# A decoder trunk step on one core: the mixer's pairs in another order, the sums of x in tiles of their own, and the first weights and last stores at other times

## The chip, the core and the metric

The kernel runs on one core of a Trainium2 chip. The core has engines that work side by side and meet at semaphores: TensorE (PE in the profile; PEld is its weight load), VectorE (DVE), ScalarE (ACT), GpSimd (POOL) and SyncE (SP). SP and POOL issue nearly all transfers; what is issued by one of them is in one queue. The metric is the time of one execution on the device in microseconds (us).

## The reference

One step of a hybrid decoder layer for 512 prompt positions and 8 sample positions, 520 columns in all:

```
proj = rmsnorm(x) @ w_in                       # 2048 -> b, c, hin, q, k, v, og, glr
cu, _ = causal_dwconv(cg * hin, conv_prev, conv_w)
ya = bg * cu                                   # 1024 channels, gated convolution
o, s_new = gla_chunked(q, k, v, logf, s0, 64)  # 4 heads, dk 128, dv 256
yb = rmsnorm_per_head(o) * silu(og)            # 1024 channels, gated attention
x = x + concat(ya, yb) @ w_out
u, v = split(rmsnorm(x) @ w_up)                # 2 x 5632
x = x + (silu(causal_dwconv(u, prev, w) + b) * v) @ w_down
y = rmsnorm(x)
```

Beside `y`, the new convolution and attention states are returned. All is float32.

## The kernel before, in words

Activations lie transposed, 128 channels by 520 columns in a tile (P = 128, T = 520, HT = 260). A float32 product is made of three matmuls on halves: `split` writes a rounded high part (ACT, L117, L105, L1166) and the rest as low part (DVE, L118, L106, L1170), and PE multiplies high by high, high by low and low by high.

The stages in order of time are these.

1. The first projections and the attention heads 0 to 3 (to about 493 us in the trace shown). Each product is a plain `group` (matmuls on L134). Beside the matmuls run the steps of the head before (`gla_head`), and in a head the gate's decay goes through ACT (L801 to L815), a scan on DVE (`bc`, L810), POOL (`e<-bc`, L227), and ACT and DVE again to `L` (L837, L840), which PE needs on L897. A scheduler orders the instructions of this stage by its own estimates.
2. Nine pairs of projection tiles, table `MIX`: `ch` is a pair of c and hin of one convolution tile, `b` two tiles of b, `og` two tiles of the gate. From here on products are made by a seven-product form (Strassen and Winograd) for blocks of two by two, products in the order `ORDER = (1, 5, 6, 2, 7, 3, 4)`. Step i is one product of 24 matmuls (`up_product`, L1190); pair n takes the steps 7n to 7n + 6, and NM = 63 is the first step of the next stage. From here on the instructions of each engine run in the order of the code.
3. "wo", the output projection: two chunks c of the 2048 input channels, four groups g of output tiles each, seven products a group (`chunk_product`, L1429; `chunk_finish` adds the products onto `acc`, on DVE at L1447, or copies on ACT at L1445).
4. "up" and "down", the feed-forward part (to about 2180 us), and the last norm.

The names the change touches:

- `mixer_sums(g)` (L665), g = 0 to 3, makes the forms 5, 4, 7, 6 of x for stage 2: four loads of x on POOL (L671, from `xT_d`), scaling on ACT (L673), sums on DVE, and a split; the result is kept (g = 0) or stored to `mt_d` by POOL (`stored`, L633). It runs beside the heads, in tiles of the pool `tmp` (eight buffers, shared with the heads). `load_mixer_sums(g)` (L694) brings the stored forms back by POOL (L697).
- `weights` (L1096) loads a pair's four weight tiles by SP: (1,1), (2,1), (2,2) at once (L1109), (1,2) later (`load_rest`, L1149). The tiles (2,k) lie in the pool `raw2`. `s` (DVE, L1112) is the first sum of two of them.
- `mixed_done` and `mix_gate` finish a pair: y tiles, their pair sums (`pair_sums`), and four stores by `stored`, which splits on ACT into a buffer `fh`, then on DVE, and then lets POOL write both halves to `g_d`. A `yield` of v in a step list means "go on at v steps after the pair's first product was followed".
- `load_form(kind, c, j)` (L615) loads the forms of product j of chunk c from `g_d`, two tiles of 260 KB for the high half (x = 0) and two for the low half (x = 1).
- `load_residual(g)` (L1395) loads the residual into `acc`; `add_residual` (L1400) adds it by accumulating transfers.
- `flat` (L577) are ten small stores of the last convolution tile's new state.

The forms of chunk 0 are loaded during the last pair, and the choice of queue is:

```python
first = kind == "wo" or c == 0 and x == 1
(nc.gpsimd if first else nc.sync).dma_start(
```

Of the kernel before, what the change touches and what calls it, by code (L numbers as in the profile page):

```python
# [9 lines left out]
F32 = mybir.dt.float32  # L10
# [3 lines left out]
ALU = mybir.AluOpType  # L14
# [23 lines left out]
def trunk_kernel(  # L38
# [565 lines left out]
    def load_form(kind, c, j):  # L604

        home = (7 * c + j) % 8
        parts_ = []
        for x in range(2):
            tiles = []
            for q in range(2):  # L610
                t = slots[2 * home + q].tile(
                    [P, T], F32R, tag=f"y{'hl'[x]}{2 * home + q}", name="form"
                )
                first = kind == "wo" or c == 0 and x == 1
                (nc.gpsimd if first else nc.sync).dma_start(  # L615
                    two(t.bitcast(F32)),
                    forms_d[kind][c][PLACE[ORDER[j]], x, 2 * q : 2 * q + 2].rearrange(
                        "i p c -> p i c"
                    ),
                )  # L620
                tiles += halves(t)
            parts_.append(tiles)
        xd[kind, c, ORDER[j]] = list(zip(*parts_))
# [41 lines left out]
    def mixer_sums(g):  # L665


        xg = [tmp()[:, :T] for _ in range(4)]
        for q, x in enumerate(xg):
            m = first_tile("mix", g, q // 2)  # L670
            nc.gpsimd.dma_start(two(x), rows_of(xT_d, "mix", g, q))  # L671
            for j, h in enumerate(halves(x)):
                nc.scalar.activation(h, h, AF.Copy, scale=gmix[:, m + j : m + j + 1])  # L673

        def out(f, t):
            if g == 0:
                split(t, *form(f, g))
            else:
                stored(t, [mt_d[f - 4, g, x] for x in range(2)], tmp())

        yield
        t1, t2 = xg[0], tmp()[:, :T]
        sub(t1, xg[0], xg[1])
        minus(t2, t1, xg[3])
        out(5, t1)
        yield
        minus(xg[2], t2, xg[2])
        out(4, t2)
        out(7, xg[2])
        yield  # L690
        sub(xg[1], xg[3], xg[1])
        out(6, xg[1])

    def load_mixer_sums(g):  # L694
        for f in (5, 4, 7, 6):
            for x, t in enumerate(form(f, g)):
                nc.gpsimd.dma_start(t.bitcast(F32), mt_d[f - 4, g, x])  # L697

    def pair_sums(he, h):

# [8 lines left out]
    with ExitStack() as mix:  # L709
# [13 lines left out]
        def mixed_done(k, y):  # L723
            if k % 2 == 0:
                return
            he, dst, i = even.pop(k - 1), g_d[k // 8], k // 2 % 4
            t21, t34 = pair_sums(he, y)
            for src, f in ((halves(he)[0], 6), (t21, 0), (t34, 2), (y, 4)):
                n = 1 if f == 6 else 2
                stored(src, [dst[f : f + n, x, i] for x in range(2)], tmp())  # L730
# [305 lines left out]
        slots[1::4] = slots[2::4] = [yt2] * 4  # L1036
        wxr = yctx.enter_context(tc.tile_pool(name="raw2", bufs=4, side="right"))
        wxp = yctx.enter_context(tc.tile_pool(name="sums", bufs=2, side="right"))
        for g in (1, 2):
            load_mixer_sums(g)  # L1040

        for j in range(2):
# [27 lines left out]

    def chunk_source(kind, w, c, g, m, k):
        c0 = first_tile(kind, g, m - 1) * P
        return w[8 * c * P : 8 * (c + 1) * P, c0 : c0 + 2 * P].rearrange(
            "(i t p) c -> t p i c", t=2, p=P
        )[k - 1]

    MIX = (
        ("ch", 4), ("ch", 5), ("b", 4), ("og", 2), ("ch", 6), ("ch", 7), ("b", 6), ("og", 4),  # L1080
        ("og", 6),
    )

    def mix_source(n, m, k):
        what, j = MIX[n]
        c0 = {"ch": 1024 * m + j * P, "b": (j + m - 1) * P, "og": 5120 + (j + m - 1) * P}[what]
        return w_in[(k - 1) * 1024 : k * 1024, c0 : c0 + P].rearrange("(k p) c -> p k c", p=P)

    def source(kind, at):
        if kind == "mix":  # L1090
# [5 lines left out]
    def weights(source, dma7):  # L1096


        raw, s = {}, wxp.tile([P, 1024], F32, tag="s", name="s", bufs=1)
        loads = []  # L1100
        for m, k in ((1, 1), (2, 1), (2, 2), (1, 2)):
            w = (wp if m == 1 else wxr).tile(
                [P, 1024], F32, tag="raw", name="raw", bufs=m + 2
            )
            src = source(m, k)
            loads.append((w.rearrange("p (k c) -> p k c", k=src.shape[1]), src))
            raw[m, k] = w
        for x in loads[:3]:
            nc.sync.dma_start(*x)  # L1109

        def plus(out, x, y):
            return lambda: nc.vector.tensor_tensor(out, x, y, op=ALU.add)  # L1112

        def dma_plus(out, x):

            return lambda: nc.gpsimd.dma_start(out, x, accum_op=ALU.add)

        src = {
            1: raw[1, 1], 2: raw[1, 2], 3: s, 4: raw[2, 2], 5: s, 6: s, 7: raw[2, 1],
        }  # L1120
        sums = {
            5: plus(s, raw[2, 2], raw[2, 1]), 6: plus(s, s, raw[1, 1]), 3: plus(s, s, raw[1, 2]),
        }
        if not dma7:
            sums[7] = plus(raw[2, 1], raw[2, 1], raw[1, 1])
        return dict(
            src=src, sums=sums, bank={}, used=set(), rest=loads[3],
            seventh=dma_plus(raw[2, 1], raw[1, 1]) if dma7 else lambda: None,
        )

# [10 lines left out]
    def begin(n):  # L1141
        kind, at = groups[n]

        state[kind, at] = weights(
            source(kind, at), kind == "up" or kind in ("mix", "wo") and at[0] > 0
        )

    def load_rest(n):
# [127 lines left out]
    def mix_gate(n):  # L1276


        st = state.pop(("mix", (n,)))
        u, v = st[2], st[7]  # L1280
        what, j = MIX[n]
        if what == "ch":
            zt = next_z()
            z = zt[:, 2 : 2 + T]
            nc.vector.scalar_tensor_tensor(z, u, -1.0, v, op0=ALU.mult, op1=ALU.mult)
            mult(z, z, R2)
            yield 1.5
# [12 lines left out]
        k = j  # L1300
        if what == "og":
            k = 8 + j
            mult(v, v, R)
            on = [tmp()[:, :T] for _ in range(2)]
            for x in range(2):
                nc.sync.dma_start(on[x], o_d[j + x])
            yield 0.5
            nc.scalar.activation(u, u, AF.Silu)
            nc.scalar.activation(v, v, AF.Silu, scale=-1.0)
            yield 3  # L1310
            mult(u, u, on[0])
            mult(v, v, on[1])
            yield 4
        dst, i = g_d[k // 8], k // 2 % 4
        t21, t34 = pair_sums(u, v)
        yield 4.5
        stored(halves(u)[0], [dst[6:7, x, i] for x in range(2)], fh())
        yield 7
        stored(v, [dst[4:6, x, i] for x in range(2)], fh())
        yield 7.5  # L1320
        stored(t21, [dst[0:2, x, i] for x in range(2)], fh())
        yield 10.5
        stored(t34, [dst[2:4, x, i] for x in range(2)], fh())

    def gate(t):
# [68 lines left out]
        for q in range(4):  # L1394
            nc.gpsimd.dma_start(two(acc[g, q]), rows_of(xT_d, "wo", g, q))  # L1395

    def add_residual(g):

        for q in range(4):
            nc.gpsimd.dma_start(  # L1400
                two(acc[g, q]), rows_of(x1_d, "down", g, q), accum_op=ALU.add
            )

    def load_last():

# [30 lines left out]
    def chunk_finish(i):  # L1436
# [3 lines left out]

        def onto(q, b, op=ALU.add):
            a = two(acc[g, q])
            if kind == "down" and c == 0 and (q, b) not in ((1, "f"), (3, "a")):
                scale = 1.0 if op == ALU.add else -1.0
                nc.scalar.activation(a, inner(bk[b]), AF.Copy, scale=scale)  # L1445
            else:
                nc.vector.tensor_tensor(a, a, inner(bk[b]), op=op)  # L1447
# [129 lines left out]
    for i, (kind, at, r) in enumerate(order):  # L1577
# [43 lines left out]
        if kind == "wo":  # L1621
# [2 lines left out]
                load_form("wo", 1, 0)  # L1624
            if c == 0 and j == 4 and g + 1 < NG:
                load_residual(g + 1)
            if c == 0 and g == NG - 1 and j >= 1:
                load_form("wo", 1, j)
            if c == 1 and g == NG - 1:
# [6 lines left out]
        if 7 * n in (NM - 7, NU - 7):  # L1636
            for x in {1: (0, 1), 2: (2, 3), 4: (4, 5), 6: (6,)}.get(j, ()):
                load_form(groups[n + 1][0], 0, x)
        if i == NM - 1:
            load_residual(0)  # L1640
        if kind == "down":
            c, g = at
            if c == 0 and g == 0 and j == 1:
# [1 line left out]
            if c == 0 and j == 0:  # L1645
                new_sums(g)
            if j == 5 and (c, g) in ((1, 0), (1, 1), (1, 2), (2, 2)):
                add_residual({0: 2, 1: 3}.get(g, c - 1))
# [143 lines left out]
```

## Time and profile before

| | |
|---|---|
| time, median of 3 runs (range) | 2253.38 us (2252.05 to 2257.63) |
| the profiled execution: its time, its span | 2252.56 us, 2250.8 us |
| busy in the span: PE, DVE, ACT, POOL | 96%, 77%, 49%, 22% |
| transfers | 426.16 MB, mean 189 GB/s |
| matmuls | 17751 |

A row of a group or of the timeline gives the start or the busy time, the line and operation, what is written and read, and in brackets how long the engine was idle before it and what ended this. "SPq" and "POOLq" are the sequencers that issue transfers. Row "x24" is 24 instructions. In a row of windows stand the stretch, its length, the busy time of PE, PEld, DVE, ACT and POOL with their counts, the granted clock of PE, the transfers' busy share and GB/s. A row of waits gives the total, the number of times and the longest, in us. In the rows of queues (q0 is POOL's, q1 SP's) stand packets, MB and the share of the 16 DMA engines. In the chain a row is start, length and what.

### The profile page before, as it was taken

Reading aid. Unit: us, or ns where it says so; the run is one execution under the profiler, and the core shown is the slowest. Engines: PE = TensorE matmul, PEld = TensorE weight load, DVE = VectorE, ACT = ScalarE, POOL = GpSimd, SP = SyncE. Lnnn points to the kernel's source line nnn. Section 1 sums busy time; section 2 is a strip of 40 time slices with the busy share of each in tenths; the row PEclk is TensorE's granted clock in tenths of the full one; section 3 lists DMA queues with packets and bytes.
Section 4 is the critical chain, followed back from the end, with each engine's and each line's share of the span. In section 5 each row is a group of like instructions: output and inputs, shape, how many; then the busy total and the mean of one; then the engine's idle time right before and its main releaser. Section 6 shows DMA issues by size and latency. Waiting matters only on the chain.

```text
span 2250.8 us, 43866 instructions
## 1 busy us (share of the span) xinstructions
PE 2171.4 (96%) x17751; PEld 2143.3 (95%) x17751; DVE 1739.4 (77%) x2290; ACT 1112.7 (49%) x1625; POOL 490.7 (22%) x687
## 2 busy tenths in 40 slices
PE   8998999989997998999999999999999999999997
PEld 7998889989997997999999999999999999999997
DVE  5365473647886897888888889888899878888876
ACT  5344453334543476655555555555555554444445
POOL 3135151341225421121221221113112311010000
PEclk9999999999998999999999999999999999999999
DMA  8344464467769799676676766766767968784734
GB/s 245 103 133 146 123 201 138 112 220 188 196 164 303 246 267 307 158 187 176 169 189 169 188 176 169 188 171 179 185 167 197 293 172 234 235 247 152 227 104 151
DMA packets 465367, 426.16 MB, mean 189 GB/s; under 512 B 22233, under 2 KB 418421, under 8 KB 465021
## 3 DMA queue, kind: packets, MB, share of 16 engines
q1 hardware_dynamic: 418193, 285.85, 44.2%
q0 software_dynamic: 45648, 135.29, 22.2%
q8 instruction: 139, 2.28, 0.4%
q10 hardware_dynamic: 1324, 2.23, 0.3%
q14 instruction: 63, 0.52, 0.1%
HBM read 304.78 MB, written 85.64 MB: 173 GB/s over the span
## 4 chain that ended last, share of the span: by engine, by line
PE 83%; DMA 6%; DVE 5%; ACT 2%; issue 2%; POOL 1%; SPq 1%; ACTq 0%; DVEq 0%; POOLq 0%
PE mm L1190 33%; PE ms L1190 13%; PE mm L134 11%; PE y L1429 8%; PE x L1429 8%; PE f L1429 3%; PE e L1429 3%; DMA t<-o_d 1%; DMA yl<-t_d 1%; DVE lo L106 1%; PE ms L897 1%; DVE lo L1170 1%; DMA vb<-v_d 1%; DMA form<-g_d 1%; DMA s<-in_state_gla_dram 1%
## 5 line engine op out<-in xcount | busy, mean ns | idle before, releaser
L1190 PE MATMUL mm<-yl,hi 128*128 128x260 f32 x1696 | 478.5, 282 | 3.5 <-DVE yl L118 2.8
L1190 PE MATMUL mm<-yh,lo 128*128 128x260 f32 x1696 | 480.1, 283 | 1.0 <-DVE lo L1170 1.0
L1190 PE MATMUL mm<-yh,hi 128*128 128x260 f32 x1696 | 479.9, 283 | 0.7 <-DMA yh<-t_d 0.5
L1166 ACT ACTIVATE hi<-raw 128x1024 fp32r<-128x1024 f32 x324 | 342.5, 1057 | 228.7 <-PE mm L1190 71.2
L1170 DVE TENSOR_TENSOR lo<-raw,hi 128x1024 fp32r<-128x1024 f32 x324 | 395.5, 1221 | 36.6 <-ACT hi L1166 36.1
L1170 DVE TENSOR_TENSOR lo<-s,hi 128x1024 fp32r<-128x1024 f32 x243 | 298.3, 1228 | 126.6 <-ACT hi L1166 121.1
L1166 ACT ACTIVATE hi<-s 128x1024 fp32r<-128x1024 f32 x243 | 257.2, 1059 | 221.3 <-DVE s L1112 85.2
L1190 PEld LDWEIGHTS mm<-yl,hi 128*128 128x128 f32 x1696 | 319.5, 188 | 4.4 <-DVE yl L118 3.0
L1190 PEld LDWEIGHTS mm<-yh,lo 128*128 128x128 f32 x1696 | 319.5, 188 | 1.2 <-DVE lo L1170 1.2
L1190 PEld LDWEIGHTS mm<-yh,hi 128*128 128x128 f32 x1696 | 319.4, 188 | 1.3 <-DMA yh<-t_d 0.7
L1190 PE MATMUL ms<-b,hi 128*128 128x260 f32 x1408 | 257.6, 283 | 0.0
L1190 PEld LDWEIGHTS ms<-b,hi 128*128 128x128 f32 x1408 | 217.8, 189 | 0.0
L1429 PE MATMUL x<-form,hi 128*128 128x260 f32 x1120 | 207.1, 285 | 10.5 <-ACT e L1453 6.9
L1429 PE MATMUL y<-form,hi 128*128 128x260 f32 x1120 | 204.6, 283 | 1.9 <-DVE acc L1447 1.9
L1112 DVE TENSOR_TENSOR s<-s,raw 128x1024 f32<-128x1024 f32 x162 | 197.8, 1221 | 2.8
L1190 PE MATMUL ms<-b,lo 128*128 128x260 f32 x704 | 198.8, 282 | 0.0
L1429 PEld LDWEIGHTS x<-form,hi 128*128 128x128 f32 x1120 | 174.1, 190 | 11.8 <-ACT e L1453 7.1
L1429 PEld LDWEIGHTS y<-form,hi 128*128 128x128 f32 x1120 | 172.4, 188 | 2.3 <-ACT hi L1166 2.3
L1429 PE MATMUL x<-form,lo 128*128 128x260 f32 x560 | 159.2, 284 | 0.0
L1429 PE MATMUL y<-form,lo 128*128 128x260 f32 x560 | 158.3, 283 | 0.0
L106 DVE TENSOR_TENSOR lo<-raw,hi 128x1024 fp32r<-128x1024 f32 x76 | 96.6, 1271 | 71.7 <-ACT hi L105 61.8
L105 ACT ACTIVATE hi<-raw 128x1024 fp32r<-128x1024 f32 x76 | 79.8, 1052 | 118.5 <-PE mm L134 112.5
(354 smaller groups left out, 5212.6 us busy)
## 6 DMA issues: line engine op xcount, KB each, us to landing
raw<-in_w_up_dram SPq DMA_DIRECT2D x176, 512.0 KB
raw<-in_w_down_dram SPq DMA_DIRECT2D x96, 512.0 KB
raw<-in_w_in_dram SPq DMA_DIRECT2D x92, 512.0 KB
form<-f_d SPq DMA_DIRECT2D x126, 260.0 KB
raw<-raw POOLq DMA_DIRECT2D x56, 512.0 KB, 5.4
f_d<-t POOLq DMA_DIRECT2D x80, 260.0 KB, 5.2
raw<-in_w_out_dram SPq DMA_DIRECT2D x32, 512.0 KB
form<-g_d POOLq DMA_DIRECT2D x56, 260.0 KB, 7.6
```

What stands on the lines that cost most here:

```text
L105: nc.scalar.activation(hi, raw, AF.Copy)
L106: nc.vector.tensor_tensor(lo, raw, hi.bitcast(F32), op=ALU.subtract)
L134: nc.tensor.matmul(o, w, xx, start=first and i == 0, stop=last and i == 2)
L897: nc.tensor.matmul(pb[:, c * 64 : (c + 1) * 64], L[:, c, :], rhs[:, c], start=True, stop=True,)
L1112: return lambda: nc.vector.tensor_tensor(out, x, y, op=ALU.add)
L1166: nc.scalar.activation(his[i], src, AF.Copy)
L1170: nc.vector.tensor_tensor(los[i], src, his[i].bitcast(F32), op=ALU.subtract)
L1190: nc.tensor.matmul(st["bank"][b], w[:, k, :], x, start=b not in st["used"] and k == 0 and j == 0, stop=k == 7 and j == 2, skip_group_check ...
L1429: nc.tensor.matmul(ps[:, m, :], w[:, k, m * P : (m + 1) * P], x, start=b not in st["used"] and k == 0 and j == 0, stop=k == 3 and j == 2, ...
```

## The change

It has these parts:

1. `MIX` goes from ch4, ch5, b4, og2, ch6, ch7, b6, og4, og6 to ch4, og2, ch5, og4, b4, og6, ch6, ch7, b6, and the gate's tiles become chunk 0 of the projection, the convolution's chunk 1 (`g_d[1 - k // 8]`, and `c = 1 - c` in `chunk_source`).
2. The four stores of the last pair come at 9.5, 13.5, 17.5 and 20.5 instead of 4.5, 7, 7.5 and 10.5.
3. The form loads of chunk 0: high halves on SP, low halves on POOL.
4. The residual of group 0 is not loaded before the first sums. Four of the six first accumulations become ACT copies; `add_residual("wo", 0)` follows in group 2.
5. `mixer_sums` uses tiles of `yt1` (name `yx`) instead of `tmp`, starts with its four loads of x, and stores all four groups; eight more stores and eight more loads.
6. `second_half` issues the two weights (2,1) and (2,2); for the first pair this happens when the pool `raw2` opens (`early`).

The core of the diff:

```diff
@@ load_form
-                first = kind == "wo" or c == 0 and x == 1
-                (nc.gpsimd if first else nc.sync).dma_start(
+                pool = x == 1 if c == 0 else kind == "wo"
+                (nc.gpsimd if pool else nc.sync).dma_start(
@@ mixer_sums
-        xg = [tmp()[:, :T] for _ in range(4)]
+        def place(n):
+            return yt1.tile([P, T], F32, tag=f"y{'hl'[n % 2]}{n // 2 * 4}", name="yx")
+        xg = [place(n) for n in range(4)]
+        for q, x in enumerate(xg):
+            nc.gpsimd.dma_start(two(x), rows_of(xT_d, "mix", g, q))
+        yield
...
-        def out(f, t):
-            if g == 0:
-                split(t, *form(f, g))
-            else:
-                stored(t, [mt_d[f - 4, g, x] for x in range(2)], tmp())
+        def out(f, t, hi):
+            stored(t, [mt_d[f - 4, g, x] for x in range(2)], hi)
...
+    def second_half(source):
+        raw = {}
+        for k in (1, 2):
+            w = raw[2, k] = wxr.tile([P, 1024], F32, tag="raw", name="raw")
+            src = source(2, k)
+            nc.sync.dma_start(w.rearrange("p (k c) -> p k c", k=src.shape[1]), src)
+        return raw
@@ after the heads
-        for g in (1, 2):
+        early = second_half(lambda m, k: mix_source(0, m, k))
+        for g in range(3):
             load_mixer_sums(g)
@@ weights
-        for x in loads[:3]:
-            nc.sync.dma_start(*x)
+        nc.sync.dma_start(*loads[0])
+        raw = {**raw, **(second or second_half(source))}
@@ mix_gate
-        dst, i = g_d[k // 8], k // 2 % 4
+        dst, i = g_d[1 - k // 8], k // 2 % 4
-        yield 4.5
+        late = n == len(MIX) - 1
+        yield 9.5 if late else 4.5
         stored(halves(u)[0], [dst[6:7, x, i] for x in range(2)], fh())
-        yield 7
+        yield 13.5 if late else 7
         stored(v, [dst[4:6, x, i] for x in range(2)], fh())
-        yield 7.5
+        yield 17.5 if late else 7.5
         stored(t21, [dst[0:2, x, i] for x in range(2)], fh())
-        yield 10.5
+        yield 20.5 if late else 10.5
         stored(t34, [dst[2:4, x, i] for x in range(2)], fh())
@@ chunk_finish
-            if kind == "down" and c == 0 and (q, b) not in ((1, "f"), (3, "a")):
+            new = kind == "down" or g == 0
+            if new and c == 0 and (q, b) not in ((1, "f"), (3, "a")):
@@ the loop over steps
+            if c == 0 and g == 2 and j == 1:
+                add_residual("wo", 0)
-        if i == NM - 1:
-            load_residual(0)
+        if i == NM:
+            new_sums(0)
```

POOL at the start of the output projection, before. `g_d_119` is chunk 0, `g_d_120` chunk 1, `acc` the residual's sums:

```order
L615 DMA form<-g_d_119 128x2x260 x16
L633 DMA g_d_119<-fh 128x2x260
L633 DMA g_d_119<-t 128x2x260
L633 DMA g_d_120<-fh 128x260
L633 DMA g_d_120<-t 128x260
L615 DMA form<-g_d_119 128x2x260 x12
L1395 DMA acc<-xT_d 128x2x260 x4
```

The same place after:

```order
L1127 DMA raw<-raw 128x1024
L615 DMA form<-g_d_119 128x2x260 x4
L577 DMA out_dram<-flat 8x128 x10
L615 DMA form<-g_d_119 128x2x260 x10
L1409 DMA acc<-xT_d 128x2x260 x4
L633 DMA g_d_120<-fh 128x260
L633 DMA g_d_120<-t 128x260
```

Half of the forms have left the queue, the last pair's stores stand behind all of them, the residual that follows them is group 1's, and the ten `flat` stores have come in between.

SP at the start of the nine pairs, before. L1109 loads (1,1), then (2,1) and (2,2); L1149 is (1,2); `t<-o_d` is an attention output for the gate:

```order
L1003 DMA o_d<-o 128x520 x2
L1109 DMA raw<-in_w_in_dram 128x8x128
L1044 DMA t<-o_d 128x520
L1109 DMA raw<-in_w_in_dram 128x8x128 x2
L1149 DMA raw<-in_w_in_dram 128x8x128
L1109 DMA raw<-in_w_in_dram 128x8x128
L1044 DMA t<-o_d 128x520
```

The same place after; L720 is `second_half`:

```order
L1027 DMA o_d<-o 128x520 x2
L1119 DMA raw<-in_w_in_dram 128x8x128
L1069 DMA t<-o_d 128x520
L1161 DMA raw<-in_w_in_dram 128x8x128
L720 DMA raw<-in_w_in_dram 128x8x128 x2
L1119 DMA raw<-in_w_in_dram 128x8x128
L720 DMA raw<-in_w_in_dram 128x8x128
L1069 DMA t<-o_d 128x520
```

The first pair's (1,2), L1161, now stands ahead of its (2,1) and (2,2), and one more weight of the second pair ahead of the second `t<-o_d`.

POOL in head 0, before; `e<-bc` begins the head's decay:

```order
L671 DMA t<-xT_d 128x2x260 x4
L227 TENSOR_TENSOR e<-bc 128x4x64 x2
L227 TENSOR_TENSOR e<-bc 128x8x32 x2
L671 DMA t<-xT_d 128x2x260 x2
L227 TENSOR_TENSOR e<-bc 128x16x16 x2
```

And after:

```order
L633 DMA mt_d<-yx 128x520
L674 DMA yx<-xT_d 128x2x260
L633 DMA mt_d<-yx 128x520 x7
L674 DMA yx<-xT_d 128x2x260 x3
L633 DMA mt_d<-yx 128x520 x3
L674 DMA yx<-xT_d 128x2x260
L633 DMA mt_d<-yx 128x520 x5
L674 DMA yx<-xT_d 128x2x260 x4
L227 TENSOR_TENSOR e<-bc 128x4x64 x2
L227 TENSOR_TENSOR e<-bc 128x8x32 x2
```

All loads and stores of two groups' sums, and the loads of more, stand ahead of the first `e<-bc`; with the four loads ahead of this piece they are 29.

More of the change, by code (lines that the diff above doesn't have):

```diff
@@ L665, in mixer_sums @@
     def mixer_sums(g):
-        xg = [tmp()[:, :T] for _ in range(4)]
+        def place(n):
[4 more added lines that the diff above has]
+        yield
         for q, x in enumerate(xg):
             m = first_tile("mix", g, q // 2)
-            nc.gpsimd.dma_start(two(x), rows_of(xT_d, "mix", g, q))
             for j, h in enumerate(halves(x)):
                 nc.scalar.activation(h, h, AF.Copy, scale=gmix[:, m + j : m + j + 1])
-        def out(f, t):
-            if g == 0:
-                split(t, *form(f, g))
-            else:
-                stored(t, [mt_d[f - 4, g, x] for x in range(2)], tmp())
+        def out(f, t, hi):
+            stored(t, [mt_d[f - 4, g, x] for x in range(2)], hi)
         yield
-        t1, t2 = xg[0], tmp()[:, :T]
+        t1, t2 = xg[0], place(4)
         sub(t1, xg[0], xg[1])
         minus(t2, t1, xg[3])
-        out(5, t1)
+        out(5, t1, place(5))
         yield
         minus(xg[2], t2, xg[2])
-        out(4, t2)
-        out(7, xg[2])
+        out(4, t2, place(6))
+        out(7, xg[2], place(7))
         yield
         sub(xg[1], xg[3], xg[1])
-        out(6, xg[1])
+        out(6, xg[1], place(5))
     def load_mixer_sums(g):
@@ L697, in load_mixer_sums, with mix_source @@
                 nc.gpsimd.dma_start(t.bitcast(F32), mt_d[f - 4, g, x])
+    MIX = (
+        ("ch", 4), ("og", 2), ("ch", 5), ("og", 4), ("b", 4), ("og", 6), ("ch", 6), ("ch", 7),
+        ("b", 6),
+    )
+    def mix_source(n, m, k):
+        what, j = MIX[n]
+        c0 = {"ch": 1024 * m + j * P, "b": (j + m - 1) * P, "og": 5120 + (j + m - 1) * P}[what]
+        return w_in[(k - 1) * 1024 : k * 1024, c0 : c0 + P].rearrange("(k p) c -> p k c", p=P)
+    def second_half(source):
[5 more added lines that the diff above has]
+        return raw
     def pair_sums(he, h):
@@ L725, in mixed_done @@
                 return
-            he, dst, i = even.pop(k - 1), g_d[k // 8], k // 2 % 4
+            he, dst, i = even.pop(k - 1), g_d[1 - k // 8], k // 2 % 4
             t21, t34 = pair_sums(he, y)
@@ L1072, in chunk_source @@
         c0 = first_tile(kind, g, m - 1) * P
+        c = 1 - c if kind == "wo" else c
         return w[8 * c * P : 8 * (c + 1) * P, c0 : c0 + 2 * P].rearrange(
@@ L1075, in chunk_source @@
         )[k - 1]
[L1079 to L1087, printed above, removed]
     def source(kind, at):
@@ L1094, in source, with weights @@
         return lambda m, k: chunk_source(kind, w_out if kind == "wo" else w_down, *at, m, k)
[L1096 to L1105, printed above, removed]
+    def weights(source, dma7, second=None):
+        s = wxp.tile([P, 1024], F32, tag="s", name="s", bufs=1)
+        raw, loads = {}, []
+        for k in (1, 2):
+            w = raw[1, k] = wp.tile([P, 1024], F32, tag="raw", name="raw")
+            src = source(1, k)
             loads.append((w.rearrange("p (k c) -> p k c", k=src.shape[1]), src))
-            raw[m, k] = w
-        for x in loads[:3]:
-            nc.sync.dma_start(*x)
+        nc.sync.dma_start(*loads[0])
+        raw = {**raw, **(second or second_half(source))}
         def plus(out, x, y):
@@ L1126, in weights @@
         return dict(
-            src=src, sums=sums, bank={}, used=set(), rest=loads[3],
+            src=src, sums=sums, bank={}, used=set(), rest=loads[1],
             seventh=dma_plus(raw[2, 1], raw[1, 1]) if dma7 else lambda: None,
@@ L1144, in begin @@
         state[kind, at] = weights(
-            source(kind, at), kind == "up" or kind in ("mix", "wo") and at[0] > 0
+            source(kind, at), kind == "up" or kind in ("mix", "wo") and at[0] > 0,
+            None if n else early,
         )
@@ L1395, in load_residual, with add_residual @@
             nc.gpsimd.dma_start(two(acc[g, q]), rows_of(xT_d, "wo", g, q))
-    def add_residual(g):
+    def add_residual(kind, g):
+        d = xT_d if kind == "wo" else x1_d
         for q in range(4):
-            nc.gpsimd.dma_start(
-                two(acc[g, q]), rows_of(x1_d, "down", g, q), accum_op=ALU.add
-            )
+            nc.gpsimd.dma_start(two(acc[g, q]), rows_of(d, kind, g, q), accum_op=ALU.add)
     def load_last():
@@ L1647, in trunk_kernel @@
             if j == 5 and (c, g) in ((1, 0), (1, 1), (1, 2), (2, 2)):
-                add_residual({0: 2, 1: 3}.get(g, c - 1))
+                add_residual("down", {0: 2, 1: 3}.get(g, c - 1))
             if c + 1 < NCD:
```

## The prediction

> **What bounds the kernel now.** I read the page first (busy shares), then what TensorE (PE) waits for, then windows around the longest waits, then the chain and the queues inside those windows.
>
> ```profile
> span 2250.8 us, 43866 instructions
> ...
> PE 2171.4 (96%) x17751; PEld 2143.3 (95%) x17751; DVE 1739.4 (77%) x2290; ACT 1112.7 (49%) x1625; POOL 490.7 (22%) x687
> ```
>
> PE is busy for 96% of the span; 2250.8 - 2171.4 = 79.4 us is all that waits can give back, beside what a reduced clock costs. The change leaves the number of matmuls as it is, so the question is which waits go. PE's longest waits (total, times, longest):
>
> ```profile
> PE mm L1190 <- DVE t L492: 8.1, 1, 8.1
> PE ms L897 <- DVE L L840: 8.1, 2, 6.0
> PE f L1429 <- DVE lo L1170: 7.2, 1, 7.2
> PE x L1429 <- ACT e L1453: 6.9, 1, 6.9
> ```
>
> The first is the start of the nine mixer pairs, the second lies in the attention heads, the last two are in the first group of the output projection. The windows (busy PE, granted clock):
>
> ```profile
> 690.00:735.00 45.00, 30.39 (x218) 29.68 (x217) 24.95 (x32) 14.83 (x20) 24.52 (x36) 0.85 0.87 288
> 930.00:1772.00 842.00, 842.00 (x7033) 842.00 (x7032) 751.38 (x1007) 459.87 (x676) 171.55 (x247) 1.00 0.68 180
> ```
>
> The second row is the undisturbed rate: 842/7033 = 0.1197 us per matmul, so a product of 24 costs 2.87 us. The first is the start of the projection: 15 us without a matmul in 45, the rest at a lower clock. These are the pieces of the chain there:
>
> ```profile
> 690.42 8.13 DMA g_d<-fh
> ...
> 710.21 8.04 DMA acc<-xT_d
> ...
> 721.38 4.32 PE f L1429 x22
> ...
> 729.32 2.87 PE y L1429 x24
> ```
>
> **The projection's start: what causes it.** The queue that issues these transfers is POOL's, and ACT's and DVE's waits show who was held:
>
> ```profile
> 673.89 3.53 POOL L615 DMA_DIRECT2D form<-g_d  x5
> ...
> 699.38 7.83 POOL L615 DMA_DIRECT2D form<-g_d  x11 [4.04 <-DMA g_d<-fh]
> 707.20 2.12 POOL L1395 DMA_DIRECT2D acc<-xT_d  x3
> ```
> ```profile
> 698.93 0.64 ACT L117 ACTIVATE fh<-t 128x520 fp32r<-128x520 f32 x1 [9.52 <-DMA g_d<-fh]
> ```
> ```profile
> DVE acc L1447 <- DMA acc<-xT_d: 10.4, 2, 8.3
> ```
>
> All 28 form loads of chunk 0 go through POOL, 0.71 us of issue each. The last pair's store, ready earlier, is issued at 690.42 behind them; its 8.13 us to landing keep ACT's next split in its buffer, and behind this split stand the copy of `e` and the next weight split, for which PE waits 6.9 us. The residual loads come after the 28th form, at 707.20; the last lands at 718.25 (710.21 + 8.04), DVE's sum waits for them, the weight remainder `lo` stands behind it, and PE waits 7.2 us.
>
> ```profile
> 689.46 0.51 PE L1429 MATMUL x<-form,hi 128*128 128x260 f32 x2 [0.48 <-ACT t L1274]
> ```
>
> This is PE's first matmul of the projection. Seven products and half a microsecond of small matmuls should take 7 x 2.87 + 0.5 = 20.6 us; the eighth product begins at 729.32 (last row of the chain), 39.9 us later. So 19.3 us are lost: 14.1 in the two long waits, 1.0 in two half-microsecond ones, about 4.2 as slow matmuls after a wait (22 in 4.32 us in place of 22 x 0.1197 = 2.63 is one such place).
>
> **What the change makes of it.** Four parts work together. (1) The gate's tiles become chunk 0, and `og6` is the sixth pair, so the last store that chunk 0's loads need falls at step 52.5, in the eighth pair, and not after the ninth; the last pair `b6` goes to chunk 1, and its stores move to steps 72.5 to 83.5, that is into the projection's second and third group, where no split of `fh` stands ahead of products 1 to 7. The first wait loses its cause. (2) The residual of group 0 is no longer loaded ahead of its sums: four of six first accumulations become ACT copies, and four accumulating transfers follow at step 78. The second wait loses its cause. ACT gets four copies in place of four additions on DVE, in a stage where ACT is busy for 14.83 of 45 us: nothing on the path. (3) The high halves move to SP, 14 issues each way. POOL then has 14 form loads, but ten stores of the transposed tile (`flat`) now stand between its fourth and fifth:
>
> ```profile
> L577 POOL DMA_DIRECT2D out_dram<-flat x10 | 5.2, 527 | 11.6 <-ACT ms L1200 11.6
> ```
>
> POOL thus has 14 x 0.71 + 5.2 = 15.1 us of issue from 674, so that the last form leaves it at 689 and lands by 697 (the 8 us seen under load); product 7, which needs it, starts at 689.5 + 6 x 2.87 = 706.7. (4) Volume: 28 x 266 KB and four weights of 512 KB are 9.5 MB. The window 690:735 moved 288 GB/s at a DMA share of 0.87; at a full share that is 331 GB/s, and 9.5 MB take 29 us: from 674 they end at 703. So the transfers just keep up with 706.7. I leave 2 us of the 19.3 for a late form: **-17.5**, with ends of -9 (a form waits 10 us, the price of the old first wait with its slow matmuls) and -19.3.
>
> **The mixer's start.** SP and POOL before the first pair:
>
> ```profile
> 479.87 1.39 SPq L1109 DMA_DIRECT2D raw<-in_w_in_dram  x2
> ```
> ```profile
> 480.83 0.55 POOL L697 DMA_DIRECT2D yh<-mt_d  x1
> ...
> 501.06 0.54 POOL L697 DMA_DIRECT2D yl<-mt_d  x1 [0.29 <-DMA yl<-mt_d]
> ```
> ```profile
> DVE s L1112 <- issue: 19.3, 1, 19.3
> ```
> ```profile
> q0 software_dynamic: 1784, 5.94, 86.7%
> q1 hardware_dynamic: 1932, 0.98, 18.8%
> ```
>
> The two second-half weights leave SP at 479.87; the first DVE sum `s` needs them and waits 19.3 us, DVE's last evacuation of the gate (L492) stands behind it, and PE waits 8.1 us, then two smaller times for `lo`:
>
> ```profile
> PE mm L1190 <- DVE lo L1170: 1.6, 2, 1.0
> PE ms L1190 <- DVE lo L1170: 1.5, 1, 1.5
> ```
>
> The rows of q0 and q1 are the transfers between 486 and 505 us: POOL's queue moved 5.94 MB, SP's 0.98, in about equally many packets (1784 and 1932). So the weights starve beside 24 loads of sums. The change issues both weights with the opening of their pool. But that memory is still held by the same earlier work, and 24 loads follow at once on POOL as before (group 0's eight are added, and are done in head 0). On SP, the pair's fourth weight (0.5 MB) now stands ahead of the two instead of behind them: up to 0.5 MB at the 288 GB/s above = 1.8 us later. I take **+2**; bounds: -11 (8.1 + 1.6 + 1.5, if the weights land first), +3.
>
> **The heads.** PE's waits of heads 1 to 3, and where head 1's longest ends and one of head 2's:
>
> ```profile
> PE ms L883 <- DVE s L870: 2.6, 3, 1.8
> PE ms L774 <- DVE v L492: 2.5, 1, 2.5
> PE ms L897 <- DVE L L840: 2.1, 1, 2.1
> ```
> ```profile
> 275.86 2.83 DVE L118 TENSOR_TENSOR t<-t 128x520 fp32r<-128x520 f32 x2 [6.62 <-ACT t L117]
> ```
> ```profile
> 195.85 0.56 POOL L633 DMA_DIRECT2D mt_d<-t  x1 [0.82 <-DVE t L118]
> ```
> ```profile
> 110.91 3.27 POOL L227 TENSOR_TENSOR e<-bc 128x256 f32<-128x256 f32 x4 [36.55 <-DVE bc L810]
> ```
>
> The sums of x are DVE, ACT and POOL work spread over heads 0 to 2; now all end in head 0. In head 2 the 2.5 us wait has two splits of sums right ahead of `v`: gone. Of the other 4.7 us there, sums stand in the way of part; I take 3. In head 1 (the 6.0 us wait) the chain runs over POOL, where the store of a sum at 195.85 with its wait takes 0.82 + 0.56 us, and DVE has a split of sums ahead of the scan that POOL waits for next (up to 2.83/2 = 1.4, taken as 1): 2.4 us. With head 2 that is -8. Against it stands head 0:
>
> ```profile
> 74.00:112.00 38.00, 38.00 (x314) 37.41 (x313) 12.92 (x20) 14.54 (x22) 1.45 (x3) 1.00 0.38 110
> ```
>
> POOL is idle for 36.55 us before `e<-bc` at 110.91, and PE is never without work there. Now 13 loads of x and 16 stores of sums stand in that gap: 13 x 0.71 + 16 x 0.56 = 18.2 us of issue and, in between, three rounds of waits for a landing, ACT's scalings and DVE's sums, which I count as 7 to 8 us each: from 71 to some 112 to 114. ACT's scalings of the third group also stand ahead of the gate's work that makes `bc`. Head 0 has no wait for `L` now (8.1 in all is head 1's 6.0 and head 2's 2.1), so there is slack; I put it at 2 us and take +2 for what goes beyond it. **-6** in all, ends -9 and +1.
>
> **Sum.** The profiled execution took 2252.56 us (span 2250.8), 0.8 below the median of the runs. 2252.56 - 17.5 + 2 - 6 = 2231.1. The later stages (up, down, last) keep their orders: nothing.
>
> **Rivals.** *The mixer's start clears too:* the 8.1 us wait and the small ones behind it go (-11 in place of +2). For it: 1.0 MB is all that is needed; against it: the gate on the memory and the equal packet shares above. 2231 - 13 = 2218; chance 0.11.
>
> *The projection's start becomes a wait for transfers.* The high forms are on SP, and the rows of 486 to 505 show SP at 0.98 MB beside POOL's 5.94. If POOL's loads are dense, the two high tiles of a product (532 KB) take 10 us at SP's 52 GB/s (0.98 MB in 19 us). POOL's 14 loads need only 3.7 MB, some 12 us at 313 GB/s, then SP has all. This costs up to 12 us of delay for what a lead of 14 us covers; a loss of 9 gives 2240. Chance 0.17. The Trainium skill ("DMA: Bandwidth & Descriptors", section "Queues, rings and completion order") says that a DMA engine takes turns between queues packet by packet; the trace's near-equal packet counts agree, and by the rule alone a queue of smaller packets loses, which is this rival.
>
> *Head 0 is pushed back, and the kernel is slower.* The 29 transfers stand ahead of `e<-bc` in POOL's order, and every microsecond that it starts after about 113 is paid in full. It decides when the block runs until about 136, so that 23 us more than my 2 are lost: its rounds, 13 to 14 us each with their issue, would have to take 21 to 22. Then 2231 + 25 = 2256. For it: a landing under load took 8.13 us, and a round has two in series; against it: the DMA share is 0.38 in the window 74:112, so that landings should be quicker. Chance 0.05.
>
> *The waits only change their name:* ACT's copies wait for products, a form or `fh` at another step, and the heads gain nothing: -4 at the projection, 2248. Chance 0.07.
>
> **How the numbers follow.** Forecast 2231, chance 0.60, own range 2225 to 2237. The range of 2219 to 2247 holds it, the transfer rival and half of the first. 0.3% (6.8 us) is what a measurement tells from no change: faster, below 2246.6, is 0.60 + 0.11 + 0.17 = 0.88, less 0.02 for tails: 0.86; same 0.08; slower 0.06.
>
> **What would show it.** Right: no wait of PE over 3 us between products 1 and 8 of the projection, granted clock near 1.00 there; no `acc<-xT_d` ahead of DVE's first sums; the wait before L774 in head 2 gone; the 8 us wait at the first pair still there. Wrong: PE waiting for `form`; `e<-bc` of head 0 after 118; the first pair starting below 496.

## The result and the profile after

The changed kernel takes 2237.3 us (median of 4 runs, 2236.34 to 2242.03) against 2253.3 us; the ratio is 0.993, with a 95% interval from 0.9911 to 0.9949. It is faster by about 16 us, where 22 were forecast. The profiled execution took 2237.56 us. Of the six executions of `ping_pong_sync` below, one took 3588.99 us at a granted clock of 0.62, where the others had 0.99; it is left out of its median.

From the page of the changed kernel (span, then busy time and share by engine), and PE's longest waits (total, times, longest):

```profile
span 2235.9 us, 43902 instructions
...
PE 2167.9 (97%) x17751; PEld 2141.5 (96%) x17751; DVE 1733.5 (78%) x2286; ACT 1114.3 (50%) x1629; POOL 487.5 (22%) x689
```
```profile
PE mm L1202 <- DVE t L492: 12.6, 1, 12.6
PE ms L798 <- DVE v L492: 7.0, 3, 6.0
PE ms L921 <- DVE L L864: 5.5, 2, 3.2
```

The two waits of 7 us in the projection are gone from the top of the list. The wait at the first pair has grown from 8.1 to 12.6 us, and a wait of 6.0 us for `v` is new. The projection's window and its chain:

```profile
690.00:735.00 45.00, 43.31 (x362) 43.13 (x362) 35.51 (x40) 19.75 (x24) 13.65 (x20) 1.00 0.81 264
```
```profile
691.65 1.69 issue
693.34 3.12 PE x L1442 x24
...
714.17 2.87 PE y L1442 x24
```

PE is busy for 43.31 of 45 us instead of 30.39, at a granted clock of 1.00 instead of 0.85. From the first product (693.34) to the eighth it takes 20.8 us in place of 39.9, with no wait between (20.7 and 39.7 by the starts of the matmuls, which is the count used below).

The new wait in head 0 starts on ACT (timelines of POOL, ACT, DVE and POOL again; in brackets the idle time before a row):

```profile
88.31 0.72 POOL L674 DMA_DIRECT2D yx<-xT_d  x1 [2.55 <-DMA mt_d<-yx]
91.60 1.43 POOL L674 DMA_DIRECT2D yx<-xT_d  x2 [2.56 <-DMA mt_d<-yx]
```
```profile
93.93 0.92 ACT L679 ACTIVATE yx<-yx,par 128x260 f32<-128x260 f32 x2 [7.16 <-DMA yx<-xT_d]
96.03 0.51 ACT L679 ACTIVATE yx<-yx,par 128x260 f32<-128x260 f32 x1 [1.19 <-issue]
96.45 1.04 ACT L105 ACTIVATE hi<-raw 128x1024 fp32r<-128x1024 f32 x1
...
113.17 1.75 ACT L679 ACTIVATE yx<-yx,par 128x260 f32<-128x260 f32 x4 [3.60 <-DMA yx<-xT_d]
116.33 0.51 ACT L679 ACTIVATE yx<-yx,par 128x260 f32<-128x260 f32 x1 [1.41 <-DMA yx<-xT_d]
116.74 0.82 ACT L825 ACTIVATE t<-ms,par 128x260 f32<-128x260 f32 x2
```
```profile
102.65 0.76 DVE L492 TENSOR_TENSOR v<-mm,R 128x260 f32<-128x260 f32 x2
```
```profile
112.33 0.71 POOL L674 DMA_DIRECT2D yx<-xT_d  x1 [2.63 <-DMA mt_d<-yx]
120.60 0.72 POOL L674 DMA_DIRECT2D yx<-xT_d  x1 [7.56 <-ACT t L830]
123.34 2.90 POOL L227 TENSOR_TENSOR e<-bc 128x256 f32<-128x256 f32 x4 [2.03 <-DVE bc L834]
```

POOL can load the next group of x only when the stores of the group before have left the same tiles (88.31 and 91.60). ACT's scaling waits 7.16 us for the first of these loads, which lands at 93.85, with the weight split (96.45) behind it; then DVE has its sums ahead of `v`. In the next round the scaling at 113 to 116 stands ahead of the gate's step L825, from which `bc`, `e` and `L` come.

Where PE comes to the first pair, and how long it waits there, of before and of after:

```profile
501.01 0.56 PE L1190 MATMUL mm<-bh,hi 128*128 128x260 f32 x1 [8.12 <-DVE t L492]
```
```profile
505.32 0.56 PE L1202 MATMUL mm<-bh,hi 128*128 128x260 f32 x1 [12.62 <-DVE t L492]
```

So PE was done with the heads at 492.89 (501.01 - 8.12) before and at 492.70 (505.32 - 12.62) after. By matching PE's matmuls of the two traces, which come in the same order, the changed kernel is 0.7 us ahead when head 0 begins, 12.1 us behind at its end and 0.2 us ahead at the end of the heads: heads 1 to 3 gained 12.3 us.

### The profile page after: what moved, and what is told of

It reads as the page before. It is cut to its first block, busy times and chain, and to the rows that moved or that the text cites. A ratio compares the mean times of both kernels' runs of the same rounds, so it can differ in the third digit from the quotient of the medians.

```text
span 2235.9 us, 43902 instructions
## 1 busy us (share of the span) xinstructions
PE 2167.9 (97%) x17751; PEld 2141.5 (96%) x17751; DVE 1733.5 (78%) x2286; ACT 1114.3 (50%) x1629; POOL 487.5 (22%) x689
## 4 chain that ended last, share of the span: by engine, by line
PE 83%; DMA 6%; DVE 4%; issue 2%; ACT 2%; SPq 1%; POOL 1%; ACTq 0%; DVEq 0%; POOLq 0%
PE mm L1202 33%; PE ms L1202 14%; PE mm L134 11%; PE x L1442 8%; PE y L1442 8%; PE e L1442 3%; PE f L1442 3%; DMA raw<-in_w_out_dram 1%; DMA yx<-xT_d 1%; PE ms L921 1%; DMA yl<-t_d 1%; DMA raw<-raw 1%; DMA t<-o_d 1%; DVE lo L106 1%; DVE lo L1182 1%
## 5 line engine op out<-in xcount | busy, mean ns | idle before, releaser
L1178 ACT ACTIVATE hi<-raw 128x1024 fp32r<-128x1024 f32 x324 | 342.4, 1057 | 230.6 <-PE mm L1202 68.5
L1202 PE MATMUL mm<-bh,hi 128*128 128x260 f32 x424 | 121.7, 287 | 15.4 <-DVE t L492 12.6
```

The costliest lines, as they stand in the source:

```text
L1178: nc.scalar.activation(his[i], src, AF.Copy)
L1202: nc.tensor.matmul(st["bank"][b], w[:, k, :], x, start=b not in st["used"] and k == 0 and j == 0, stop=k == 7 and j == 2, skip_group_check ...
```

## The experiments

Twelve kernels, each the changed kernel with one edit, or with two joined. The time of the changed kernel moves by some us from run to run, so times that differ by under 3 us are not told apart here; stages are compared by the trace. In the eight kernels with the heads of the changed kernel, PE is done with the heads between 489.7 and 494.3 us, so this reading does not tell 5 us apart; most of the spread lies ahead of head 0.

### The sums of x

`old_sums` puts the sums back as they were:

```diff
-        xg = [place(n) for n in range(4)]
+        xg = [tmp()[:, :T] for _ in range(4)]
...
+            if g == 0:
+                split(t, *form(f, g))
...
-        for g in range(3):
+        for g in (1, 2):
```

> The changed kernel with the sums of x as they were before (tiles of the pool tmp, group 0 kept in place, three groups stored). Theory A: the sums cost head 0 about 12 us and give heads 1 to 3 about 12 us, so that without this part both go: PE's waits of 6.0 us (for v) and 3.2 us (for L) in head 0 vanish, the 6.0 us wait for L in head 1 and those of 2.5, 2.1 and 1.8 us in head 2 come back, and the time stays at 2237 within 3 us. Rival B: the heads gain from something else than the sums (other transfers moved); then head 0 gets better and heads 1 to 3 stay good, and the time falls to about 2225.

Measured: 2239.92 us (2237.12 to 2245.41), ratio 0.9931 [0.9914, 0.9948]. PE's waits from 70 to 400 us:

```profile
PE ms L919 <- DVE L L862: 9.1, 2, 6.0
PE ms L905 <- DVE s L892: 4.0, 3, 2.3
PE ms L796 <- DVE v L492: 2.4, 1, 2.4
```

The waits of before are back in heads 1 and 2, those of 6.0 us for `v` and 3.2 us for `L` in head 0 are gone, and PE is done with the heads at 494.66. This is Theory A: the part of the change that moves the sums gives as much as it takes.

`sums_pinned` spreads them in time and keeps their new tiles:

```diff
         for q, x in enumerate(xg):
-            nc.gpsimd.dma_start(two(x), rows_of(xT_d, "mix", g, q))
+            d = nc.gpsimd.dma_start(two(x), rows_of(xT_d, "mix", g, q))
+            tc.add_manual_dep(d.ins, last, ...)   # last: POOL's last instruction so far
```

> The changed kernel with its own tiles for the sums, but the four loads of each group bound to their place in the code on POOL, so that they start behind the first e<-bc of head 0 and run beside heads 0 to 3. Theory A1: heads 1 to 3 lost time to the sums only because these shared the tiles of tmp and stood in front of the heads' steps as a block; with own tiles and early loads both costs stay small: head 0 loses under 3 us, heads 1 to 3 under 4, and the time falls by 7 to 11 us to 2226 to 2230. Rival A2: it is the sums' work on DVE, ACT and POOL itself, wherever it stands, that delays the heads: waits of 6 to 12 us come back in heads 1 to 3, and the time stays within 4 us of 2237.

Measured: 2251.68 us (2248.84 to 2256.33), ratio 0.9981 [0.9973, 0.999].

```profile
PE ms L929 <- DVE L L872: 15.6, 3, 8.2
PE ms L806 <- DVE v L492: 6.3, 1, 6.3
```

Rival A2 holds, and more strongly than it said: PE is done with the heads at 507.19, 14.5 us later than in the changed kernel. New tiles do not make the sums free in heads 1 to 3.

`ping_pong` takes away the wait for the stores: two sets of four tiles for the loads, in turn, with the other sums in tiles of `tmp`, which the heads use too.

```diff
+            if n > 3:
+                return tmp()[:, :T]
+            n += g % 2 * 4
             return yt1.tile([P, T], F32, tag=f"y{'hl'[n % 2]}{n // 2 * 4}", name="yx")
```

> The changed kernel with the eight tiles used as two sets of four for the loads of x, in turn, and the other sums in tiles of tmp. The loads of two groups can go at once, and no load waits for the stores of the group before it. Theory M: head 0 loses its 6.0 us (PE waits for v) and 3.2 us (for L) because ACT's scalings, which wait for such late loads, stand in front of the weight splits and of the gate's work; both waits fall under 2 us, and since two groups now end in heads 1 and 2, waits of 2 to 5 us come back there: the time falls by 3 to 9 us against 2237. Rival N: it is the amount of sums' work that counts; what head 0 wins the later heads lose, and the time stays within 3 us.

Measured: 2239.5 us (2235.59 to 2242.0), ratio 0.9934 [0.9914, 0.9953].

```profile
PE ms L924 <- DVE L L867: 9.9, 6, 3.3
PE ms L910 <- DVE s L897: 5.5, 3, 3.0
```

The 6.0 us wait for `v` is gone, as Theory M says of the mechanism, but the waits are now many small ones, spread over the heads, and PE is done with the heads at 495.92. On the time, Rival N is right.

`sums_unmade` leaves the sums out:

```diff
-        xg = [place(n) for n in range(4)]
...
+        x = place(g)
+        nc.gpsimd.dma_start(two(x), rows_of(xT_d, "mix", g, 0))
+        yield
+        for f in (5, 4, 7, 6):
+            for d in range(2):
+                nc.gpsimd.dma_start(mt_d[f - 4, g, d], x)
```

> The changed kernel with the sums of x left out: each group loads one tile and stores it eight times, so that the stores to mt_d and their loads stay, and ACT's scalings and splits, DVE's sums and splits and twelve of the sixteen loads go. It tells what the sums cost the heads wherever they stand. Theory N (price conserved, from ping_pong): the sums' own work on ACT and DVE costs the heads about 12 us in every placing tried; without it head 0 and heads 1 to 3 are both free of waits over 2.5 us, and the time falls by 10 to 13 us to 2224 to 2227. Rival O: the heads wait for one another's steps and transfers anyhow; waits of over 5 us in all stay in the heads, and the time falls by under 6 us.

Measured: 2230.34 us (2229.01 to 2231.17), ratio 0.9896 [0.9882, 0.9909].

```profile
PE ms L903 <- DVE L L846: 5.7, 2, 3.4
```
```profile
496.49 0.56 PE L1184 MATMUL mm<-bh,hi 128*128 128x260 f32 x1 [14.66 <-DVE t L492]
```

PE is done with the heads at 481.83, 10.9 us before the changed kernel; of this 7 us reach the end, since the wait at the first pair is 2 us longer and other waits later. The price in the heads is as Theory N has it, but not the time (7 us in place of 10 to 13); waits of 7 us in all for `L` and `s` stay, as Rival O says.

The heads can be compared more closely, between the same matmuls: from PE's first 500 matmuls to its first 1000 (head 0; 83 to 161 us in the changed kernel), and from there to the end of the heads. The eight kernels with the same heads take 78.0 to 79.1 and 330.8 to 332.2 us for these.

| kernel | head 0, us | heads 1 to 3, us |
|---|---|---|
| before | 65.6 | 343.8 |
| changed | 78.3 | 331.5 |
| `old_sums` | 65.8 | 345.9 |
| `sums_pinned` | 67.0 | 358.2 |
| `ping_pong` | 67.8 | 344.2 |
| `sums_unmade` | 66.2 | 331.5 |

So making the sums, with twelve of their sixteen loads, costs the changed kernel 12.1 us, and all of it in head 0. Of the four orders that were tried, three cost the same within 3 us and the pinned one 13 to 15 us more. Why the price is so alike in head 0 and in heads 1 to 3 is not shown. A wait of 3.4 us for `L` stays in head 0 even without sums; there 44 transfers stand ahead of `e<-bc` on POOL, but `e<-bc` waits for `bc` last (1.44 us, starting at 111.51), so that they are not shown to be its cause.

### The start of the pairs

`weights_late` undoes the early issue of (2,1) and (2,2):

```diff
-        early = second_half(lambda m, k: mix_source(0, m, k))
...
-            None if n else early,
+            None,
```

> The changed kernel without the early issue of the first pair's weights (2,1) and (2,2): SP's order is as before, (1,2) behind them. Theory C: the wait at the first pair grew from 8.1 to 12.6 us because the fourth weight (1,2) went ahead of these two; the wait falls to 8 to 9 us, the time by 3 to 4 us. Rival D: the wait is set by the 24 loads of sums on POOL alone, and its growth is chance of their timing: it stays at 12 us within 1.5 and the time within 2 us.

Measured: 2238.01 us (2233.89 to 2241.86), ratio 0.9926 [0.9908, 0.9943]. PE's waits from 470 to 540 us:

```profile
PE mm L1201 <- DVE t L492: 6.7, 1, 6.7
PE ms L1201 <- DVE lo L1181: 2.3, 1, 2.3
```

The wait is 6.7 us. In the nine profiles with the early issue and with these loads on POOL it was 12.5 to 17.4. So the early issue made the wait longer, as Theory C says. The time does not show it: four runs that spread over 8 us, with 3 of the 6 us given back by 540 us, in part by longer waits for `lo` (2.9 us in place of 1.8).

`sums_by_sync` moves the 24 loads of the sums of groups 1 to 3 behind these weights on SP, in the order in which the forms are used:

```diff
+        load_mixer_sums((0,))
+        load_mixer_sums((1, 2), nc.sync)
...
-    load_mixer_sums(3)
+    load_mixer_sums((3,), nc.sync)
```

> The changed kernel with the 24 loads of sums of groups 1 to 3 at the first pair moved from POOL's queue to SP's, behind the pair's first weights, in the order of the forms' use. Theory E: the two weights starve because two queues share the engines packet by packet; behind each other they land 3 to 5 us after their issue at 480, DVE's sum runs by 486, and PE's wait of 12.6 us falls under 3 us: the time falls by 9 to 13 us to 2224 to 2228. Rival F: the bytes themselves are the limit (7.4 MB between 480 and 503 us): PE then waits for the forms or for the next weights instead, 6 us or more, and the time falls by under 6 us.

Measured: 2236.11 us (2234.7 to 2236.28), ratio 0.991 [0.9897, 0.9924]. The first matmul of the pairs, and what PE and DVE wait for next:

```profile
495.03 0.36 PE L1203 MATMUL mm<-bh,hi 128*128 128x260 f32 x1 [1.05 <-DVE t L492]
```
```profile
PE mm L1203 <- DMA yh<-mt_d: 3.6, 1, 3.6
PE mm L1203 <- DVE lo L1183: 2.4, 2, 1.5
```
```profile
DVE s L1124 <- DMA raw<-in_w_in_dram: 4.6, 1, 4.6
```

The wait falls from 12.6 to 1.05 us, as Theory E says. The weights come earlier, if not as early as it says: DVE's sum `s` starts at 493.32 in place of 503.61, and not by 486. Then PE waits for a form, and DVE for the second pair's weights, which now stand behind 24 loads; PE starts the pairs 10.3 us earlier, and by 540 us 5.6 of these are left. Rival F is right on the time.

`sums_staged` therefore puts form 7 behind the second pair's weights:

```diff
+        load_mixer_sums((1, 2), (5, 4, 6), nc.sync)
...
+        if i == 0:
+            load_mixer_sums((1, 2, 3), (7,), nc.sync)
```

> As sums_by_sync (loads of the sums on SP behind the first pair's weights), but with the forms of the last product (form 7) behind the second pair's weights, which came too late there (DVE waited 4.6 us for them, PE 1.5 to 2.7 us). If the order of the queue is what was left, the waits of PE between 493 and 540 fall from 7.1 to under 5 us, the second pair's wait under 1 us, and the time is 2 to 4 us below sums_by_sync, at about 2233 where that stands at 2236; if the bytes are the limit, PE waits for form 7 or 6 instead and the time is that of sums_by_sync within 2 us.

Measured: 2232.67 us (2229.91 to 2238.25), ratio 0.9909 [0.9893, 0.9925].

```profile
PE mm L1203 <- DVE lo L1183: 1.3, 2, 0.9
PE mm L1203 <- DMA yh<-mt_d: 1.2, 1, 1.2
PE mm L1203 <- DVE t L492: 1.0, 1, 1.0
```

DVE still waits 4.2 us for the second pair's weights, but PE's wait for `lo` behind it, 1.5 us in `sums_by_sync`, is gone. PE's waits of the stretch are 4.0 us in all, and at 540 us it is 8.1 us ahead of the changed kernel. The ratio is that of `sums_by_sync`. Both medians lie below the changed kernel's, but the intervals overlap with its own, so that a gain over it is likely and not shown.

`ping_pong_sync` joins the edits of `ping_pong` and `sums_by_sync`:

> The two sets of tiles together with the loads of sums on SP's queue behind the first weights (as in sums_by_sync). If the two act at different places, the gains add up: by Theory M 7 to 13 us below 2237, at 2224 to 2230; by Rival N 2230 to 2236, as sums_by_sync alone.

Measured: 2236.61 us (2231.92 to 2239.95), ratio 0.9918 [0.9897, 0.9939], where `sums_by_sync` alone has 0.991. Nothing adds up, as Rival N has it, because `ping_pong` gives nothing.

### The projection

`mix_before` has the pairs in the old order and the old chunks:

```diff
-        ("ch", 4), ("og", 2), ("ch", 5), ("og", 4), ("b", 4), ("og", 6), ("ch", 6), ("ch", 7),
-        ("b", 6),
+        ("ch", 4), ("ch", 5), ("b", 4), ("og", 2), ("ch", 6), ("ch", 7), ("b", 6), ("og", 4),
+        ("og", 6),
...
-        late = n == len(MIX) - 1
+        late = False
```

> The changed kernel with the pairs in the old order, the conv tiles as chunk 0 again and the last pair's stores at their old steps; forms on two queues, the late residual and the new sums stay. Theory G: the old stalls at the projection's start came mostly from this part: b6's store of chunk 0 stands among chunk 0's form loads and ACT's split for it waits on its buffer; from PE's first projection matmul to the start of its eighth product it takes 27 to 32 us instead of 20.7, with a wait of 5 us or more, and the time rises by 6 to 11 us over 2237. Rival H: with half of the forms off POOL and no residual in front, the store leaves in time; the stretch stays under 23 us and the time within 2 us of 2237.

Measured: 2250.4 us (2246.51 to 2255.91), ratio 0.9981 [0.9972, 0.999]. From the first product to the eighth it takes 35.2 us. PE's wait, DVE's, and the chain:

```profile
PE f L1441 <- DVE lo L1181: 12.5, 1, 12.5
```
```profile
DVE t L1245 <- DMA t<-o_d: 14.8, 1, 14.8
```
```profile
706.48 12.66 DMA t<-o_d
```

Theory G has the direction, and the stretch grows by more than it says (14.5 us), but the cause is another. The last pair is `og6` here; its attention outputs `t<-o_d` stand on SP behind 14 high forms and four weights and are issued at 706.48. DVE waits for them, `lo` behind it, and PE. ACT's wait for the buffer of its splits is also back (6.6 us in all), but does not reach PE. So in this kernel the old order and the high forms on SP get in each other's way; what the order alone is worth, with all forms on POOL, was not run.

`stores_early` undoes only the last pair's late stores (`late = False`):

> The changed kernel with the last pair's stores at 4.5, 7, 7.5 and 10.5 as for every pair, the rest as changed. Theory G2: POOL is free of form loads by about 700, so that the stores leave as they are made; only the shared buffer of the splits could hold ACT: the stretch of seven products grows by 0 to 2 us. Rival H2: ACT's splits wait for the buffer, of which there is more than one but whose stores take 8 us to land, and hold the copies of the first products: 4 to 7 us more.

Measured: 2236.96 us (2233.64 to 2239.55), ratio 0.992 [0.9902, 0.9938]; the seven products take 20.6 us. Theory G2 is right: the late stores are worth nothing beside the rest.

`forms_pool` has all form loads on POOL:

```diff
-                pool = x == 1 if c == 0 else kind == "wo"
+                pool = kind == "wo" or c == 0 and x == 1
```

> The changed kernel with all 28 form loads of chunk 0 on POOL again. Issue is then 28 x 0.71 + 5.2 = 25 us behind the last pair's second product. Theory I: the last form leaves at about 704 and lands at 711, where its product starts at 711: PE waits 0 to 3 us, and the time stays within 3 us of 2237. Rival J: the forms come one by one too late and the loads of the residual of group 1 behind them hold DVE, as before the change: waits of 6 us or more, the time 8 us up.

Measured: 2242.66 us (2239.09 to 2244.67), ratio 0.9944 [0.9924, 0.9965]; the stretch is 24.3 us, and the time 5.4 us up with overlapping intervals. PE's waits in 690 to 735:

```profile
PE x L1442 <- DMA form<-g_d: 2.0, 2, 1.3
PE x L1442 <- issue: 1.7, 1, 1.7
PE f L1442 <- DMA form<-g_d: 0.8, 1, 0.8
```

Theory I is right on the kind and size of the wait (2.8 us for forms), not on the time (within 3 us); the second queue is worth 3.7 us of the stretch.

`residual_first` loads the residual first and adds all of it on DVE:

```diff
-            new = kind == "down" or g == 0
+            new = kind == "down"
...
-        if i == NM:
-            new_sums(0)
+        if i == NM - 1:
+            load_residual(0)
```

> The changed kernel with the residual of group 0 loaded before its first sums as before the change, and all of these sums on DVE. POOL has 14 form loads and the flat stores before it, so the four loads leave at about 694 and land at 700 to 702. Theory K: the first sum is due when the first product is done, at 697, and DVE waits 3 to 5 us, which the weights' lead of two products hides in most part: PE waits 0 to 2 us. Rival L: DVE's weight remainder stands behind the wait, as before the change, and PE waits 5 us or more.

Measured: 2239.4 us (2236.26 to 2241.27), ratio 0.993 [0.9914, 0.9947]; the stretch is 24.7 us. DVE waits 6.4 us for `acc<-xT_d`, and one wait of 2.2 us for `lo` reaches PE, with slow matmuls behind it:

```profile
DVE acc L1461 <- DMA acc<-xT_d: 6.4, 2, 5.2
```

That lies near Theory K: the later residual is worth 4 us of the stretch. No edit alone gives back the 19 us; the largest is the order of the pairs. The four stretches grow by 14.5, 0, 3.7 and 4.0 us, together 22.2, which is more than 19.0: the parts do not simply add, and how the gain divides among them is not shown.

## Why the prediction was right and where not

**The projection's start: right.** The term was -17.5. The seven products take 19.0 us less, and a wait of 1.7 us ahead of the first product, where 0.5 stood, takes 1.2 of it: -17.8. The kernel in the old order has not got this wait, the three others with one part undone have. The two causes named, the store's wait and the residual's, went. That they were the causes is read from the two traces; put back one at a time, neither brings back its 7 us on PE (ACT's 6.6 us wait in `mix_before` does not reach PE, and in `residual_first` 2.2 us do). POOL's last form left at 696.5 and not at 689, as the `flat` stores were held up among the forms, but product 7 was late enough to hide it. In the prediction's 19.3, one of the two half-microsecond waits stands ahead of the first matmul and not in the stretch; the sum is not changed by it. Of the parts called harmless or useful, the late stores turned out to be needless. That the high forms share SP with other loads came up only where the order was undone.

**The mixer's start: right, the size in part by luck.** The term was +2, worked out from the fourth weight ahead of the two; the wait grew by 4.5 us, another of 1.5 us went, which was not counted, and PE was 2.7 us late at 520. `sums_by_sync` shows that the loads on POOL held these weights up: with 24 of them behind the weights, `s` starts 10.3 us earlier. That the queues share by equal numbers of packets is read from 1784 and 1932 before; in the changed kernel it is 1525 and 3009 between 486 and 505 us, so that equal counts are no rule here. The Trainium skill ("DMA: Bandwidth & Descriptors", section "Queues, rings and completion order") says that a DMA engine takes turns between queues by packet; the fall of the wait from 12.6 to 1.05 us agrees with it, without showing that the packet is the unit.

**The heads: wrong, and this is nearly the whole miss.** The step that failed is "-8, and +2 for head 0, together -6". The gain in heads 1 to 3 was 12.3 us, more than the 8: the waits there fell by 9.6 us, from 13.2 to 3.6, head 1's long wait from 6.0 to 2.3 us, where 2.4 had been counted for it, and all of head 2's went, 6.4 us, where 5.5 had been counted; the rest is in matmuls that follow each other more closely. The cost in head 0 was 12.1 us and not 2. The working looked at POOL's queue and asked when `e<-bc` would start. For POOL it was right: sixteen stores and twelve loads were through at 113.0, where 112 to 114 was estimated. But the thirteenth load came at 120.60, behind ACT, and `e<-bc` started at 123.34, behind `bc`, which is also later than the 118 named as the sign of an error. And the larger wait came earlier: ACT's scaling stands ahead of the weight split, and a late load there holds DVE and `v`. That ACT's scalings stand ahead of the gate's work was said, but no time was put on it. With 0 in place of -6, the sum gives 2237.1, where the profiled execution took 2237.56.

The direction was right, by the largest of its terms, and the time lies in the range, just above the 2225 to 2237 named as the forecast's own. The rival whose waits only change their name was put at 2248, which leaves out the +2 of the mixer's start; with it the sum is 2250.6.

## What to carry to other kernels

When work is moved into an idle stretch of one queue, go through every engine that the work touches and ask what stands behind each of its instructions there: a wait for a load costs whatever is queued behind the waiting instruction, not only what waits for its result. Side work that delayed three stages may cost the same in the one to which it is moved; leave it out once, to see its price, before looking for a place. At a seam between stages, take the order of the queues first: here loads that were needed first came late when bulk loads ran beside them on another queue, or when they stood behind work of a pair that had not finished; look also at what waits next, since about half of the 10.3 us that `sums_by_sync` freed went into the waits behind.

## What the runs showed that was not expected

In the three kernels that load the sums by SP, the long feed-forward stage ran at a slightly lower rate. These are the windows of the changed kernel and of `sums_staged` (length, then PE's busy time and its matmuls):

```profile
930.00:1730.00 800.00, 800.00 (x6691) 800.00 (x6691) 715.00 (x959) 436.17 (x643) 161.53 (x232) 1.00 0.69 179
```
```profile
930.00:1730.00 800.00, 800.00 (x6671) 800.00 (x6670) 711.81 (x955) 435.94 (x643) 161.22 (x232) 1.00 0.68 179
```

It is 6671 against 6691 matmuls in 800 us of work without a gap, 0.3%, or about 2.4 us over the stage, with the granted clock given as 1.00 in both. All three had 6671, and eight of the eleven others 6691, the rest 6682 or 6683; the whole stage took 901.9 to 903.2 us in the three and 899.1 to 901.1 in the others. This took back some 2.4 of the 8.1 us that `sums_staged` had gained. Its cause stays open.
